# Mixing sublayer: gate, projection and q/k, v/g products with token blocks as the stationary operand

## The chip, the core and the metric

One core of a Trainium2 chip runs the whole program: two decoder layers over 256 tokens with a model width of 1024. The metric is the time of one execution on the device in microseconds; a lower one is better. The core has a TensorE (PE, with its weight loads as PEld), a VectorE (DVE), a ScalarE (ACT), a GpSimd (POOL) and a SyncE (SP), which here only sends off the loads.

## What is computed

Each layer is a token-mixing sublayer and a mixture of experts, each followed by a norm. Cut to what matters here:

```python
z = h @ w_in[l]                      # 1024 -> 10 blocks of 256 columns and 4 gate blocks of 1024
(sc_b, sc_c, sc_x, lru_x, sg_u, sg_v, r_q, r_k, r_v, r_g, *gate_logits) = split(z)
branches = (short_conv(sc_b, sc_c, sc_x), rg_lru(lru_x),
            spatial_gating(sg_u, sg_v), retention(r_q, r_k, r_v, r_g))   # each 256 tokens x 256
merged = 0
for b in range(4):
    merged = merged + sigmoid(gate_logits[b]) * (branches[b] @ branch_proj[l, b])   # 256 -> 1024
mix = merged @ w_out[l]              # 1024 -> 1024
h = layer_norm(ALPHA * h + mix)
h = layer_norm(ALPHA * h + mixture_of_experts(h))    # 32 experts, 2 for a token
```

All of it is in float32. The kernel splits each operand of the mixing products in a leading part (hi) and a rest (lo) and sums three products: hi by hi, hi by lo and lo by hi (`tripled`, lines 328 to 330).

## The kernel before

**Weights and pieces.** The weights lie in memory in chunks of 1 MB (128 partitions by 2048 floats), in the order of use: ten input blocks (q, k, lx, v, g, sv, su, c, x, b), then four rounds of four gate chunks, one chunk of branch projections and, from the second round on, one chunk of the output projection; 34 chunks in a layer, followed by 96 chunks for the experts. SP loads each with one instruction (the first two with four) into a ring of 22 slots of 1 MB, as slots come free; the ring also holds the larger buffers of the sublayer. A chunk is used in four pieces of 512 columns. `do_split` copies a piece to `whi` on ACT and takes the rest to `wlo` on DVE (lines 256 and 257, in `hilo`), four pieces ahead of its products (`LOOK`); `wlo` has four places, so that the split of piece u+4 waits until the products of piece u are done.

**Products.** A piece of an input block or a gate takes 12 matmuls of 256 columns. For q, k, v, g and sv the tokens are stationary (128 tokens by 128 inputs) and 256 weight columns are streamed. For lx, su, c, x, b, the gates and the branch projections the weights are stationary (128 inputs by 128 channels) and the 256 tokens are streamed, so that the result has channels on the partitions. In the output projection the merged rows are stationary and 512 weight columns are streamed (`add_to`).

**Side work.** After each piece `advance` takes one step of every generator that runs beside the products: retention (`g_ret`), the recurrence (`g_lru`), spatial gating (`g_sgu`), the short convolution (`g_sc`), the merge (`g_merge`). What a step sends to PE stands in PE's order behind that piece. Each engine works its instructions off in the order in which the program gives them. Retention starts when q is done: rotations on DVE, an add on POOL, transposes on PE, scores, a standardisation (`std64`) whose inverse root is 12 small POOL instructions in three rounds of four (lines 315 to 318), two POOL products (lines 620 and 621) and, four steps later, the transposes `rtp` (line 628). Spatial gating has the same kind of `std64`, one POOL product (line 697) and then 16 matmuls `sv` (line 705).

**Merge.** For eight blocks of 128 channels and two pairs of branches, a gate bank goes through a sigmoid on ACT (line 401), the projection's bank is multiplied with it on DVE (line 483), and the two pairs are added on POOL (line 488). The sum, with channels on the partitions, is split in hi and lo and is the stationary operand of the output projection as it stands. `residual` scales `h` on POOL beside the gates (line 922; in the second layer lines 927 to 930, after a load of 1 MB), and `g_router` follows with line 291.

Of the kernel before, what the change touches and what calls it, by code (L numbers as in the profile page):

```python
# [39 lines left out]
# columns of the pack of shape constants  # L40
# [13 lines left out]


def _stream():
    s = [("in", n) for n in ("q", "k", "lx", "v", "g", "sv", "su", "c", "x", "b")]
    for m in range(4):
        s += [("gate", 2 * m + j, bp) for j in range(2) for bp in range(2)]
        s.append(("proj", m))  # L60
        if m:
            s.append(("out", m - 1))
    return s + [("out", 3)]


STREAM = _stream()
NMIX = len(STREAM)
# [15 lines left out]
class Ring:  # L83
    """The slots of 1 MB: weights in flight, and the larger buffers while they live."""
# [14 lines left out]
    def pump(self):  # L99
        while self.next < len(self.chunks) and self.free > self.reserve():  # L100
# [3 lines left out]
            if self.next % NCH == NCH - 1:  # L104
                for c in (slice(0, 1024), slice(1024, 2048)):
                    self.k.nc.sync.dma_start(t[:, c], self.chunks[self.next][:, c])
            elif self.next == 0:
                for i in range(4):
                    c = slice(512 * i, 512 * i + 512)
                    self.k.nc.sync.dma_start(self.k.xT[:, 2 * i:2 * i + 2], self.k.a["xT"][:, 2 * i:2 * i + 2])  # L110
                    self.k.nc.sync.dma_start(t[:, c], self.chunks[0][:, c])
            else:
                n = 4 if self.next == 1 else 1
                for i in range(n):
                    c = slice(2048 // n * i, 2048 // n * (i + 1))
                    self.k.nc.sync.dma_start(t[:, c], self.chunks[self.next][:, c])
# [7 lines left out]
class Kern:  # L124
    def __init__(self, ctx, tc, a, out):
# [11 lines left out]
        self.ring.chunks = []  # L137
        for l in range(L):
            self.ring.chunks += [a["mixw"][l, i] for i in range(NMIX)]
            self.ring.chunks += [a["exps"][l, g, i] for g in range(8) for i in range(12)]  # L140
# [42 lines left out]
    def rope_tables(self):  # L183
        """cos, and -sin with sin, of the angles brought to within pi of 0."""
# [69 lines left out]
    def hilo(self, hi, lo, src, eng=None):  # L254
        """hi: the leading bits of src, lo: the rest, exactly."""
# [3 lines left out]
    def params(self, l):  # L259
        """The smaller parameters of a layer's mixers."""  # L260
# [19 lines left out]
    def g_router(self, l):  # L280
        """The norm's gain and bias go into the router's weights and biases; the sums of its weights."""
# [23 lines left out]
    def rsqrt(self, v, n, tag):  # L305
        """v ** -0.5 on [P, n], by Newton's iteration."""
# [16 lines left out]
    def tripled(self, out, pairs, stop_last=True, first=True):  # L323
        """Sum of products of split operands: (lhsT hi, lo), (rhs hi, lo)."""
# [7 lines left out]
    def prologue(self, l):  # L332
        self.base, self.late = l * NCH, None
        self.pieces = [(self.base + c, s) for c in range(NMIX) for s in range(4)]
        self.splits, self.nsplit = {}, 0

    def do_split(self, u, eng=None):
# [8 lines left out]
        if s == 3:  # L346
# [3 lines left out]
    def mixer(self, l):  # L350
# [12 lines left out]
        for kind, *args in STREAM:  # L363
            n = args[0]
            if kind == "in":
                tm = n in TOKENS_FIRST
                bank = self.bank("B", "z")
                for s in range(4):
                    wh, wl = self.splits.pop(u)
                    if tm:  # L370
# [19 lines left out]
            elif kind == "gate":  # L390
                bank = self.bank("B", "z")
                for s in range(4):
                    wh, wl = (x.rearrange("p (k c) -> p k c", k=4) for x in self.splits.pop(u))
                    o = bank[:, (s // 2) * 256:(s // 2) * 256 + 256]
                    self.tripled(o, [((wh[:, kk], wl[:, kk]), hk(4 * (s % 2) + kk)) for kk in range(4)],
                                 stop_last=s % 2 == 1, first=s % 2 == 0)
                    u += 1
                    if s == 3:
                        j, bp = args
                        g = self.late_sub("gate")  # L400
                        nc.scalar.activation(g, bank, AF.Sigmoid)  # L401
                        self.gates[j, bp] = g
                        if (j, bp) == (0, 0):
                            self.residual(l)
                            self.gens.append(self.g_router(l))
                        if (j, bp) == (4, 0) and l:
                            ring.give()
                        if (j, bp) == (7, 1):
                            ring.give(2)
                    self.advance()  # L410
                    self.do_split(u - 1 + LOOK)
            elif kind == "proj":
                for s in range(4):
                    wh, wl = (x.rearrange("p (b k c) -> p b k c", b=2, k=2) for x in self.splits.pop(u))
                    j, bp = 2 * n + s // 2, s % 2
                    bank = self.bank("P", "pj")
                    for b in range(2):
                        bh, bl = (x[:, 2 * bp + b] for x in self.br)
                        self.tripled(bank[:, b * 256:b * 256 + 256],
                                     [((wh[:, b, k], wl[:, b, k]), (bh[:, k], bl[:, k])) for k in range(2)])  # L420
                    u += 1
                    self.mgens.append(self.g_merge(j, bp, bank))
                    self.advance()
                    self.do_split(u - 1 + LOOK)
                if n == 3:
                    ring.give(2)
            else:
                if self.W is None:
                    assert not self.gens
                    self.W = [[self.bank("W", "acc") for _ in range(2)] for _ in range(2)]  # L430
                def add_to(t, half, k, w):
                    mh, ml = self.merged[k]
# [913 lines left out]
```

## Time and profile before

| what | value |
|---|---|
| median of 3 runs | 863.62 us (863.32 to 863.98) |
| the profiled execution, first to last instruction | 860.7 us |
| around it: the median less that span | 2.9 us |
| PE busy | 791.3 us, 92% of the span |
| DVE busy | 386.0 us |
| ACT busy | 317.3 us |
| loads | 281.07 MB, mean 327 GB/s |
| TensorE's mean granted clock | 0.970 of full speed |

The profile is of one execution; its span leaves out what lies ahead of the first and behind the last instruction. A matmul's listed duration holds its way through the array, so that the listed times of neighbours overlap; what a matmul costs in a stream is the distance from its start to the next one's. The granted clock is a share of full speed: 1.00 is 2.4 GHz and 0.50 is 1.2 GHz.

### The profile page before, as it was taken

To read this page: it belongs to the slowest core of one execution; us is meant where nothing else is said; L and a number is where in the kernel's file an instruction comes from. 1 tells how busy PE (TensorE), PEld (TensorE's weight loads), DVE (VectorE), ACT (ScalarE), POOL (GpSimd) and SP (SyncE) were. 2 spreads that over 40 slices of the span, in tenths; PEclk is the share of its full clock that TensorE was granted. 3 is DMA by queue.
4 is the path that set the end of the run, shared out by engine and by line. 5 is a ranking of instruction groups with operands and counts; after the bars stand their busy time and mean duration, and the time that the engine had idled before them with its cause. 6 is when DMAs were issued, how large, how long until landed. Compare 5 with 4: busy or idle time off the path is not lost.

```text
span 860.7 us, 15923 instructions
## 1 busy us (share of the span) xinstructions
PE 791.3 (92%) x6438; PEld 604.1 (70%) x6438; DVE 386.0 (45%) x732; ACT 317.3 (37%) x636; POOL 124.8 (14%) x153
## 2 busy tenths in 40 slices
PE   8999999999999999867889998999999999979794
PEld 7998999999656555422389988999995565544342
DVE  5778677466621111110386779665674211111004
ACT  6564444444523211110356633544444131112012
POOL 4526211011000000000131437110010000000001
PEclk9999999999999999988999999999999999997898
DMA  9986735557799999999997474555587999999994
GB/s 346 425 354 264 253 122 179 191 196 280 323 424 426 426 426 425 425 421 425 424 425 303 158 281 164 183 196 191 175 334 320 426 426 426 425 426 427 423 425 175
DMA packets 40823, 281.07 MB, mean 327 GB/s; under 512 B 4588, under 2 KB 4588, under 8 KB 7456
## 3 DMA queue, kind: packets, MB, share of 16 engines
q1 hardware_dynamic: 40320, 279.20, 80.9%
q8 instruction: 54, 0.88, 0.4%
q10 hardware_dynamic: 288, 0.52, 0.2%
q0 software_dynamic: 128, 0.19, 0.1%
q14 instruction: 33, 0.27, 0.1%
HBM read 278.85 MB, written 1.05 MB: 325 GB/s over the span
## 4 chain that ended last, share of the span: by engine, by line
PE 58%; DMA 27%; DVE 7%; ACT 2%; POOL 1%; issue 1%; SPq 0%; DVEq 0%; ACTq 0%; POOLq 0%
DMA w<-in_exps_dram 25%; PE z L328 9%; PE z L330 9%; PE z L329 9%; PE gu L1052 6%; PE xg L1151 3%; PE y L1102 3%; PE acc L1089 3%; DVE wlo L257 2%; PE pj L330 2%; PE pj L328 2%; PE pj L329 2%; PE acc L328 2%; PE acc L329 2%; PE acc L330 2%; DMA par<-in_par_dram 2%
## 5 line engine op out<-in xcount | busy, mean ns | idle before, releaser
L257 DVE TENSOR_TENSOR wlo<-w,whi 128x512 fp32r<-128x512 f32 x269 | 215.7, 825 | 115.7 <-ACT whi L256 71.6
L330 PE MATMUL z<-hThi,wlo 128*128 128x256 f32 x672 | 192.2, 286 | 3.2 <-DVE wlo L257 3.0
L328 PE MATMUL z<-hThi,whi 128*128 128x256 f32 x672 | 192.5, 286 | 0.4 <-ACT whi L256 0.4
L329 PE MATMUL z<-hTlo,whi 128*128 128x256 f32 x672 | 191.3, 285 | 0.0
L256 ACT CAST whi<-w 128x512 fp32r<-128x512 f32 x272 | 151.4, 618 | 13.4 <-PE z L329 6.7
L1052 PE MATMUL gu<-w,xg 128*32 128x512 f32 x1024 | 128.0, 635 | 22.2 <-PEq L1175 13.0
L330 PEld LDWEIGHTS z<-hThi,wlo 128*128 128x128 f32 x672 | 130.1, 194 | 4.9 <-DVE wlo L257 4.9
L328 PEld LDWEIGHTS z<-hThi,whi 128*128 128x128 f32 x672 | 130.3, 194 | 1.2 <-ACT whi L256 0.7
L329 PEld LDWEIGHTS z<-hTlo,whi 128*128 128x128 f32 x672 | 130.2, 194 | 0.2
L1052 PEld LDWEIGHTS gu<-w,xg 128*32 128x32 f32 x1024 | 30.4, 114 | 98.2 <-issue 65.3
L1157 ACT ACTIVATE xg<-xg,cst 128x128 f32<-128x128 f32 x64 | 25.8, 454 | 167.2 <-PE xg L1151 163.9
L1159 DVE TENSOR_SCALAR xg<-xg,cst 128x128 f32<-128x128 f32 x64 | 23.3, 405 | 129.7 <-PE xg L1151 129.7
L1102 PE MATMUL y<-w,hidT 128*32 128x256 f32 x1024 | 65.4, 383 | 12.8 <-ACT hidT L1082 10.8
L1151 PEld LDWEIGHTS xg<-oh,h 128*128 128x128 f32 x512 | 59.6, 191 | 24.4 <-issue 22.7
L1089 PE MATMUL acc<-y,ct 128*128 128x256 f32 x256 | 68.1, 398 | 1.0 <-ACT y L1106 1.0
L1151 PE MATMUL xg<-oh,h 128*128 128x128 f32 x512 | 65.4, 281 | 0.0
L1089 PEld LDWEIGHTS acc<-y,ct 128*128 128x128 f32 x256 | 44.7, 189 | 25.0 <-issue 11.9
L1102 PEld LDWEIGHTS y<-w,hidT 128*32 128x32 f32 x1024 | 28.9, 109 | 41.1 <-ACT hidT L1082 14.6
L488 POOL TENSOR_TENSOR late<-late 128x512 f32<-128x512 f32 x16 | 25.9, 1616 | 203.9 <-DVE late L483 184.7
L1128 DVE TENSOR_TENSOR ow<-oh,wt 128x256 f32<-128x256 f32 x16 | 6.8, 424 | 106.9 <-PE y L1102 78.8
L1106 ACT COPY y<-y 128x256 f32<-128x256 f32 x64 | 23.8, 373 | 78.6 <-PE y L1102 78.6
L401 ACT ACTIVATE late<-z 128x512 f32<-128x512 f32 x32 | 19.1, 597 | 90.6 <-PE z L330 90.6
(257 smaller groups left out, 1044.4 us busy)
## 6 DMA issues: line engine op xcount, KB each, us to landing
w<-in_exps_dram SPq DMA_DIRECT2D x190, 1024.0 KB, 19.5
w<-in_mixw_dram SPq DMA_DIRECT2D x66, 1024.0 KB, 8.0
w<-in_mixw_dram SPq DMA_DIRECT2D x8, 256.0 KB, 6.2
par<-in_par_dram SPq DMA_DIRECT2D x2, 1024.0 KB, 15.9
w<-in_exps_dram SPq DMA_DIRECT2D x4, 512.0 KB, 17.7
xT<-in_xT_dram SPq DMA_DIRECT2D x4, 256.0 KB, 5.4
h<-in_xtok_dram SPq DMA_DIRECT2D x1, 1024.0 KB, 18.2
gb<-in_fgb_dram SPq DMA_DIRECT2D x1, 1024.0 KB, 5.8
```

The lines of the kernel that those rows point to most:

```text
L256: self.nc.scalar.copy(hi, src)
L257: (eng or self.nc.vector).tensor_sub(lo, src, hi.bitcast(F32))
L328: nc.tensor.matmul(out, ah, bh, start=first and i == 0, stop=False, skip_group_check=True)
L329: nc.tensor.matmul(out, ah, bl, start=False, stop=False, skip_group_check=True)
L330: nc.tensor.matmul(out, al, bh, start=False, stop=stop_last and i == n - 1, skip_group_check=True)
L488: nc.gpsimd.tensor_add(a, a, pr)
L1052: nc.tensor.matmul(bank[32 * c:32 * c + 32], xg[g][k // 4][:, k % 4, 32 * c:32 * c + 32], w[:, c], start=k == 0, stop=k == 7, skip_group_c ...
L1089: nc.tensor.matmul(self.W[t][half][:, c0:c0 + 256], ct[:, t * P:t * P + P], y, start=g == 0 and c0 == 0, stop=g == 7, skip_group_check=True)
L1102: nc.tensor.matmul(bank[32 * c:32 * c + 32], hidT[:, f * P + 32 * c:f * P + 32 * c + 32], w[:, f, c], start=f == 0, stop=f == 1, skip_grou ...
L1106: nc.scalar.copy(ys[q], bank)
L1151: nc.tensor.matmul(bank[:, i * P:i * P + P], self.h[:, t, k * P:k * P + P], oh[:, t].rearrange("p e s -> p (e s)"), start=t == 0, stop=t == 1)
L1157: nc.scalar.activation(x[:, 2 * j + i], bank[:, i * P:i * P + P], AF.Identity, bias=b, scale=g)
```

## The change

The order of the work is written out as a list of units (`_work`), apart from the order in memory, which stays as it is. q and k are one product, and so are v and g: for each of the 8 blocks of 128 inputs the tokens are stationary and 512 columns (256 of each) are streamed. The gates and branch projections do the same with 512 channels of one branch: two halves of the 1024 channels, in each the four branches one after the other, with two chunks of gates and half a chunk of projections each. The four gated projections of a half are added up with tokens on the partitions; then eight blocks are transposed on PE, split in hi and lo, and are the stationary operand of the output projection. Output chunk 0 comes after branch 0 of the second half, the other three at the end. Since a chunk in use now mixes columns of several chunks in memory, `parts` cuts its load: four loads of 256 KB with rows of 1 KB (q/k, v/g) or 512 B (gates), eight of 128 KB with rows of 512 B (projections). Input blocks and gates use the PSUM banks in another order, and the ring's slots are given back at other places.

```diff
-    s = [("in", n) for n in ("q", "k", "lx", "v", "g", "sv", "su", "c", "x", "b")]
-    for m in range(4):
-        s += [("gate", 2 * m + j, bp) for j in range(2) for bp in range(2)]
...
+NAMES = ("qk", "qk", "lx", "vg", "vg", "sv", "su", "c", "x", "b")
...
+    for n, name in enumerate(NAMES):
+        j = NAMES[:n].count(name)
+        work.append((("in", name, j), use("in", name, j)))
+    for hf in range(2):
+        for b in range(4):
+            for kh in range(2):
+                work.append((("gate", hf, b, kh), use("gate", hf, b, kh)))
+            two = (b % 2 * 2, b % 2 * 2 + 1)
+            work.append((("proj", hf, b), use("proj", hf, b // 2, pieces=two)))
+            if (hf, b) == (1, 0):
+                work.append((("out", 0), use("out", 0)))
+    for n in range(1, 4):
+        work.append((("out", n), use("out", n)))
...
+    def parts(self, t, u):
...
+        if kind == "in" and x in PAIRS:
+            at = STREAM.index(("in", x[0]))
+            src = mix[at:at + 2].rearrange("n p (k c) -> p k n c", k=8)[:, 4 * arg[0]:4 * arg[0] + 4]
+            dst = t.rearrange("p (k n c) -> p k n c", k=4, n=2)
+            return [(dst[:, k], src[:, k]) for k in range(4)]
...
+        if kind == "gate":
+            b, kh = arg
+            at = STREAM.index(("gate", 4 * x, b // 2))
+            src = mix[at:at + 4].rearrange("j p (b k c) -> p b k j c", b=2, k=8)[:, b % 2, 4 * kh:4 * kh + 4]
+            dst = t.rearrange("p (k j c) -> p k j c", k=4, j=4)
+            return [(dst[:, k], src[:, k]) for k in range(4)]
...
+        for (kind, n, *args), pieces in WORK:
+            if kind == "in" and n in PAIRS or kind == "gate":
+                kh = args[-1]
+                if kh == 0:
+                    banks = [self.bank("B", "z") for _ in range(2)]
+                for s in range(4):
+                    w = self.splits.pop(u)
+                    k = 4 * kh + s
+                    for t in range(2):
+                        self.tripled(banks[t], [(ht(k, t), w)], stop_last=k == 7, first=k == 0)
+                    u += 1
+                    if k == 7 and kind == "in":
+                        self.z[n] = banks
+                        self.side(l, n)
+                    elif k == 7:
+                        g = self.gates[args[0]] = [self.gate_sub(args[0], t) for t in range(2)]
+                        for t in range(2):
+                            nc.scalar.activation(g[t], banks[t], AF.Sigmoid)
+                        if (n, args[0]) == (0, 0):
+                            self.residual(l)
+                            self.gens.append(self.g_router(l))
...
+                    self.advance()
+                    self.do_split(u - 1 + LOOK)
...
+            elif kind == "proj":
+                b, = args
+                w = [self.splits.pop(u + k) for k in range(2)]
+                banks = [self.bank("P", "pj") for _ in range(2)]
+                for t in range(2):
+                    self.tripled(banks[t], [([x[:, b, k, t * P:t * P + P] for x in self.br], w[k]) for k in range(2)])
+                u += 2
+                self.mgens.append(self.g_merge(n, b, banks))
+                for i in range(2):
                     self.advance()
+                    self.do_split(u - 2 + i + LOOK)
...
+    def g_merge(self, hf, b, banks):
...
+        g = self.gates.pop(b)
+        for t in range(2):
+            nc.vector.tensor_mul(g[t], banks[t], g[t])
+            if b == 0:
+                continue
+            (nc.vector if b == 3 else nc.gpsimd).tensor_add(self.sums[t], self.sums[t], g[t])
...
+        if b < 3:
             return
...
+        yield
+        mT = [self.bank("B" if hf else "W", "mT") for _ in range(2)]
+        for t in range(2):
+            for i in range(4):
+                nc.tensor.transpose(mT[i // 2][:, i % 2 * 256 + t * P:i % 2 * 256 + t * P + P],
+                                    sums[t][:, i * P:i * P + P], self.ident)
+        yield
+        for i in range(2):
+            h, l = store[:, 2 * i], store[:, 2 * i + 1]
+            self.hilo(h, l, mT[i])
...
-        for i, n in enumerate("qk"):
-            z = yield from self.wait(n)
-            A, B = r0[2 * i], r0[2 * i + 1]
...
+        for t, z in enumerate(self.z["qk"]):
+            A, B = r0[2 * t], r0[2 * t + 1]
...
-        yield from self.wait("v")
+        yield from self.wait("vg")
...
-        yield from self.wait("g")
```

## Rows read from the trace of the kernel before

**Rows 1.** Windows: us, busy time (instructions) of each engine, PEclk, DMA share, GB/s.

```profile
100.00:200.00 100.00, 100.00 (x793) 98.08 (x792) 61.24 (x94) 45.92 (x89) 9.69 (x6) 1.00 0.52 176
225.00:235.00 10.00, 8.74 (x71) 5.27 (x73) 5.96 (x34) 5.52 (x10) 0.00 (x0) 1.00 0.58 244
250.00:336.00 86.00, 82.18 (x760) 46.60 (x756) 11.98 (x32) 19.32 (x51) 0.00 (x0) 1.00 1.01 426
```

**Rows 2.** Groups by line and shape on PE: busy us, mean ns, idle before.

```profile
L328 PE MATMUL z<-hThi,whi 128*128 128x256 f32 x672 | 192.5, 286 | 0.4 <-ACT whi L256 0.4
...
L328 PE MATMUL z<-whi,hThi 128*128 128x256 f32 x160 | 47.9, 299 | 2.3 <-ACT whi L256 1.5 <-DVE lru L650 0.7
...
L328 PE MATMUL pj<-br,whi 128*128 128x256 f32 x128 | 36.2, 283 | 0.0
```

**Rows 3.** Timeline of PE, gates: start us, us, engine, line, operation.

```profile
100.08 0.28 PE L330 MATMUL z<-hThi,wlo 128*128 128x256 f32 x1
...
103.80 0.28 PE L328 MATMUL z<-hThi,whi 128*128 128x256 f32 x1
```

**Rows 4.** Timeline of PE, output projection.

```profile
142.30 0.40 PE L328 MATMUL acc<-whi,late 128*128 128x512 f32 x1
...
144.81 0.39 PE L330 MATMUL acc<-whi,late 128*128 128x512 f32 x1
```

**Rows 5.** Timelines of PE, ACT and DVE where a projection follows a gate.

```profile
135.84 0.28 PE L328 MATMUL pj<-br,whi 128*128 128x256 f32 x1
...
136.04 0.60 ACT L401 ACTIVATE late<-z 128x512 f32<-128x512 f32 x1 [3.10 <-PE z L330]
...
137.18 0.69 DVE L257 TENSOR_TENSOR wlo<-w,whi 128x512 fp32r<-128x512 f32 x1 [1.83 <-ACT whi L256]
137.79 0.68 DVE L483 TENSOR_TENSOR late<-pj,late 128x512 f32<-128x512 f32 x1
```

**Rows 6.** Timeline of PE, four transposes and the next product.

```profile
456.38 0.60 PE L584 MATMUL rtp<-cst,ret 128*128 128x128 f32 x4
456.73 0.36 PE L328 MATMUL z<-whi,hThi 128*128 128x256 f32 x1
```

**Rows 7.** Timeline of POOL, two of the six rounds of the inverse roots.

```profile
60.21 0.51 POOL L315 TENSOR_TENSOR rzr<-ryr 128x8 f32<-128x8 f32 x1 [1.84 <-DVE ryr L312]
...
62.03 0.71 POOL L318 TENSOR_TENSOR ryr<-ryr,rzr 128x8 f32<-128x8 f32 x1
...
75.13 0.20 POOL L315 TENSOR_TENSOR rzs<-rys 128x8 f32<-128x8 f32 x1
...
75.98 0.20 POOL L318 TENSOR_TENSOR rys<-rys,rzs 128x8 f32<-128x8 f32 x1
```

**Rows 8.** Timelines of DVE and PE, and a window (PE busy, PEclk, DMA).

```profile
62.60 0.68 DVE L535 TENSOR_REDUCE sas<-sgu 128x8 f32<-128x512 f32 x1
...
73.78 0.66 PE L628 MATMUL rtp<-cst,ret 128*128 128x128 f32 x4 [2.10 <-POOL ret L621]
...
74.00:80.00 6.00, 6.00 (x45) 0.72 0.25 101
```

**Rows 9.** Timelines of POOL, DVE and PE beside the residual's scaling, both layers.

```profile
84.54 5.75 POOL L922 TENSOR_SCALAR h<-h 128x2048 f32<-128x2048 f32 x1
...
84.97 4.73 DVE L257 TENSOR_TENSOR wlo<-w,whi 128x512 fp32r<-128x512 f32 x2
...
520.29 15.29 DVE L257 TENSOR_TENSOR wlo<-w,whi 128x512 fp32r<-128x512 f32 x9
...
532.27 0.38 PE L330 MATMUL z<-hThi,wlo 128*128 128x256 f32 x1 [1.10 <-DVE wlo L257]
```

**Rows 10.** Timelines of PE and ACT, start of the second layer.

```profile
430.37 0.47 PE L328 MATMUL z<-whi,hThi 128*128 128x256 f32 x1
...
436.99 3.93 ACT L256 CAST whi<-w 128x512 fp32r<-128x512 f32 x7
...
438.69 0.39 PE L329 MATMUL z<-wlo,hThi 128*128 128x256 f32 x1 [0.66 <-DVE wlo L257]
```

More of the change, by code (lines that the diff above doesn't have):

```diff
@@ L53, with _work, use @@
 TOKENS_FIRST = ("q", "k", "v", "g", "sv")
+PAIRS = ("qk", "vg")
+NAMES = ("qk", "qk", "lx", "vg", "vg", "sv", "su", "c", "x", "b")
 def _stream():
     s = [("in", n) for n in ("q", "k", "lx", "v", "g", "sv", "su", "c", "x", "b")]
-    for m in range(4):
-        s += [("gate", 2 * m + j, bp) for j in range(2) for bp in range(2)]
[L60 to L63, printed above, removed]
+    for hf in range(2):
+        s += [("gate", 4 * hf + j, bp) for bp in range(2) for j in range(4)]
+        s += [("proj", 2 * hf + m) for m in range(2)]
+    return s + [("out", n) for n in range(4)]
+def _work():
+    s, work, at = [], [], {}
+    def use(*key, pieces=range(4)):
+        if key not in at:
+            at[key] = len(s)
+            s.append(key)
+        return [(at[key], i) for i in pieces]
+    for n, name in enumerate(NAMES):
+        j = NAMES[:n].count(name)
+        work.append((("in", name, j), use("in", name, j)))
+    for hf in range(2):
+        for b in range(4):
[7 more added lines that the diff above has]
+        work.append((("out", n), use("out", n)))
+    return s, work
 STREAM = _stream()
+LOADS, WORK = _work()
 NMIX = len(STREAM)
@@ L103, in pump @@
             t = self.take("w")
[L104 to L111, printed above, removed]
-            else:
[L113 to L116, printed above, removed]
+            dma = self.k.nc.sync.dma_start
+            parts = self.k.parts(t, self.next)
+            if self.next == 0:
+                for i, (dst, src) in enumerate(parts):
+                    dma(self.k.xT[:, 2 * i:2 * i + 2], self.k.a["xT"][:, 2 * i:2 * i + 2])
+                    dma(dst, src)
+            else:
+                for dst, src in parts:
+                    dma(dst, src)
             self.tiles[self.next] = t
@@ L333, in prologue @@
         self.base, self.late = l * NCH, None
-        self.pieces = [(self.base + c, s) for c in range(NMIX) for s in range(4)]
-        self.splits, self.nsplit = {}, 0
+        self.pieces = [(self.base + c, s) for _, pieces in WORK for c, s in pieces]
+        self.splits, self.nsplit, self.whole = {}, 0, {}
     def do_split(self, u, eng=None):
@@ L345, in do_split @@
         self.splits[u] = hi, lo
-        if s == 3:
+        self.whole[c] = self.whole.get(c, 0) + 1
+        if self.whole[c] == 4:
             del self.ring.tiles[c]
@@ L362, in mixer @@
         u = 0
[L363 to L367, printed above, removed]
+        tags = {"lx": "P", "sv": "P", "su": "B", "c": "P", "x": "B", "b": "P"}
+        for (kind, n, *args), pieces in WORK:
[19 more added lines that the diff above has]
+                            self.gens.append(self.g_router(l))
+                        if (n, args[0]) == (1, 0) and l:
+                            ring.give()
+                        if (n, args[0]) == (1, 3):
+                            ring.give(2)
+                    self.advance()
+                    self.do_split(u - 1 + LOOK)
+            elif kind == "in":
+                bank = self.bank(tags[n], "z")
                 for s in range(4):
                     wh, wl = self.splits.pop(u)
-                    if tm:
+                    if n == "sv":
                         wh, wl = (x.rearrange("p (k c) -> p k c", k=2) for x in (wh, wl))
@@ L389, in mixer @@
                     self.advance()
[L390 to L409, printed above, removed]
-                    self.advance()
[L411 to L426, printed above, removed]
@@ new lines, in mixer @@
+            elif kind == "proj":
[7 more added lines that the diff above has]
+                for i in range(2):
+                    self.advance()
+                    self.do_split(u - 2 + i + LOOK)
+                if (n, b) == (1, 3):
+                    ring.give()
@@ L456, in mixer @@
                     self.advance()
-        assert not self.splits
+        assert not self.splits and not self.mgens
         next(norm, None)
@@ L460, in mixer @@
         self.needs[l] = int(l + 1 == L)
-        ring.give(3)
+        ring.give(4)
     def advance(self):
@@ L515, in side @@
             self.gens.append(self.g_sc(l))
-        elif n == "v":
-            self.nc.scalar.copy(self.r1[2], self.z["v"])
-        elif n == "g":
+        elif n == "vg":
+            for t in range(2):
+                self.nc.scalar.copy(self.r1[2][:, 256 * t:256 * t + 256], self.z["vg"][t][:, :256])
             self.gens.append(self.g_silu())
```

85 lines of the change are left out of this document (46 added, 39 removed).

## The prediction

> **What bounds the kernel now.** First the windows, for the stages. In the middle of a mixing sublayer PE is busy for the whole 100 us at full clock, while DMA has 0.52 of its time taken: the sublayer goes at PE's pace. Between sublayer and experts DMA falls to 0.58 because the ring is full; from 250 us on it is at 1.01 and 426 GB/s and PE waits for it [rows 1]. So the experts' stage starts when the sublayer's PE work ends, with a full ring, and then takes a fixed number of bytes: what a sublayer gains or loses on PE moves the end by the same amount, once a layer. Next the groups by shape and the timeline of PE, for what a product costs; then DVE, ACT and POOL at the places where PE would have to wait for them.
>
> **What the streaming saves.** Of the 672 products of a kind with weights stationary, 512 belong to gates (16 chunks of 16, two layers), the other 160 to lx, su, c, x and b, which stay. Of the 160 with tokens stationary, 128 belong to q, k, v and g. With the 128 projections that makes 768 of each of three kinds [rows 2], 2,304 products of 256 columns, which become 1,152 of 512. In a stream a product of 256 columns takes (103.80 - 100.08) / 31 = 0.120 us [rows 3], one of 512 columns with its own stationary load takes (144.81 - 142.30) / 11 = 0.228 us [rows 4]. The sum is 2,304 x 0.120 - 1,152 x 0.2282 = 276.5 - 262.9 = **13.6 us saved**; a piece goes from 1.44 to 1.37 us. The other number of columns is not an extrapolation: the output projection already runs in this shape.
>
> The Trainium skill speaks against it: TensorE: Matmul & The Clock Gate, Back-to-back issue gap, gives an isolated product N / 2.4 + 2.5 ns, by which a pair of 256 costs 218 ns and one of 512 costs 216. By that only 1,152 x 2.5 ns = 2.9 us would be saved and the sum below would end 10.7 us higher. The rows show 240 against 228, and I go by them.
>
> **What the merge adds.** Before, the sums came out with channels on the partitions and PE never waited for them. Now 8 transposes for each half stand in PE's order directly behind the last projection of the half, and they need both gated sums. Four transposes hold up the next product by 456.73 - 456.38 = 0.35 us [rows 6]. For the wait I set the start of a projection at 0, by the place where one follows a gate now [rows 5]: it starts at 135.84, the sigmoid 0.20 later, the next split's copy behind it, its subtraction on DVE at 1.34, the first gate product at 1.95. The first of the two sigmoids now waits for a bank that ends 0.68 earlier, so that the second one keeps this place. DVE then has: product 1.95, add 2.66, product 3.27, add 3.98 to 4.67 (0.68 each, 0.03 more where one needs the other). PE ends its 12 products at 2.74, starts the first four transposes at 3.45, the second four at 4.77 and is free at 5.12. So each merge costs 5.12 - 2.74 = 2.4 us, 1.7 of it waiting; four of them **9.5 us**. At best DVE has no split ahead and the chain starts when the first bank is done, at 1.6: 2.0 us each, 8 in all. At worst a POOL instruction slows one of the DVE operations, as it does elsewhere (0.69 to 1.7 us, [rows 5, 9]): 3.4 each, 13.6 in all. I take 9.5, as POOL is idle there. What is queued behind the transposes is the next gate or output piece, whose split is already made; it loses nothing more. The other merges (branches 0 to 2) are the same two DVE products and two POOL adds with a gate's 11 us to spare.
>
> **What moves: retention.** Before, its scores came after v, at step 17; now after v and g, at step 21, and everything of it that follows comes four pieces later. Its inverse root then falls on the same steps (31 to 33) as that of spatial gating, and POOL works six rounds in one row. A round took 2.53 us where DVE was busy (60.21 to 62.74) and 1.05 where it was not (75.13 to 76.18) [rows 7]; I take 1.75, near the middle, 10.5 us for six. Before, PE waited 2.10 us at `rtp`, until 73.78; so piece 36 ended at 71.68, and by 1.44 us a piece piece 30 ended at 63.0 and piece 27 at 58.7, while gating's reduction for step 27 ran at 62.60, DVE being 3.9 late [rows 8]. Without retention's part ahead of it DVE is some 2 us late, 1.1 us have been saved by then, and two reductions of 0.68 come first: the rounds run from 63.0 - 1.1 + 2 + 1.4 = 65.3 to 75.8, gating's product on POOL ends some 0.7 later (an estimate, less than half such a round), and `sv`, whose place is behind piece 38 at 71.68 + 2.88 - 1.1 = 73.5, waits for it **3.0 us** in place of the 2.1 at `rtp`, which now comes late enough. Both waits are followed by a lower clock: 0.72 over 6 us, for a part of them the 1.2 GHz of the two levels, 1.7 us lost [rows 8]. So I count **+1.0 us a layer, 2.0**. Bounds: all rounds at 1.05 leave no wait and no fall of the clock (-3.8 a layer); all at 2.53 give 15.2 and a wait of 7.7 (+5.6 a layer).
>
> **What moves: the residual.** While POOL scales `h`, a split on DVE takes 2.4 us (first layer) or 1.7 us (second) instead of 0.69 [rows 5, 9]. In the first layer POOL starts as soon as its queue is empty, as before, but retention's last subtraction now lies in that stretch: 2.4 us of DVE more, of which I take half to be covered by the pieces split ahead: **+1.3**. In the second the load is sent off four pieces later, so that the stretch holds a merge (two products, 1.4 us) and 11 splits that are needed 0.07 us sooner each: **+2.2** on top of waits like the one of 1.10 us now [rows 9]. Bounds: 0, if the lookahead covers all, to 7.
>
> **The start of the second layer.** A piece now needs only one block of `hT` and lasts 1.37 us, so PE doesn't run out of them; but the fourth split is needed after three blocks instead of six: 430.37 + 3 x 1.37 = 434.5, and its copy still starts at 436.99, its rest is ready at 438.69 [rows 10]. PE stands for 3 us or more at once and then has five pieces left where it had five already; the 0.5 us saved are outweighed by a fall of the clock as at `rtp` (1.7): **+1.2**, between -0.5 and 1.7.
>
> **At nothing:** the loads in short rows and their many more issues (SP does nothing else, DMA has 48% free in this stage [rows 1]); the other PSUM banks; the four large hi/lo splits for eight small ones; projection chunks and one buffer held longer in a ring that is full anyway. If that cover is gone, the third rival is the price.
>
> **Sum:** -13.6 + 9.5 + 2.0 + 3.5 + 1.2 = +2.6 us: a profiled span of 863.3 for 860.7 and, with 2.9 us around it, **866.2 us** for the median of 863.6.
>
> **Rivals.**
> 1. *POOL is in time* (faster). One place, the inverse roots: nothing else wants DVE while they run, so that the rounds go at the quick rate. It decides if six rounds and gating's product take under 8 us (1.2 a round). Then neither `sv` nor `rtp` waits and the clock stays: 866.2 - 2 x (3.0 + 1.7) = 856.8. For it: rounds of 1.05 and DVE less behind than before; against: rounds of 2.53, and two reductions that now fall together [rows 7, 8].
> 2. *The clock falls at the merges too* (slower): 4 x 1.7 = 6.8 on top, 873.0. Against it: the waits are two short ones, 0.7 and 1.0 us, not one of 2.1 [rows 8].
> 3. *The short rows starve PE* (slower). A gate chunk is used up in 24 x 0.228 = 5.5 us, and at 426 GB/s 1 MB takes 2.5. The free 48 us of 100 [rows 1] spread over the 20 cut chunks of that stage leave 4.9 us for each; at 5.5 us (190 GB/s) the lack is 12 us a layer, 890. The Trainium skill (DMA: Bandwidth & Descriptors, Rules for kernel authors) asks for 1 MB or more in one load for full bandwidth, and these are 128 to 256 KB; no row shows such a load in this stage.
> 4. *The streaming saves nothing* because a product of 512 with its load costs two of 256 here: 879.8. The rows of the output projection speak against it [rows 4]. By the rule of the Trainium skill above it would be 876.9.
>
> **How the numbers follow.** Forecast (own range 861 to 870) 0.43; rival 1 0.31; rival 2 0.15; rival 3 0.06; rival 4 0.05. A measurement of this kernel can tell about 0.2% (1.7 us) from no change. Faster: rival 1 and 0.06 of the forecast's lower end, 0.37. Same (861.9 to 865.3): 0.18, all of the forecast. Slower: the forecast's other 0.19 and rivals 2 to 4, 0.45. The range, 855 to 876, takes in rivals 1 and 2 and leaves out most of 3 and 4.
>
> **What would show it.** Products of 512 columns 0.228 apart; at four places PE's transposes wait for DVE's add, some 1.7 us each; one wait of 2 to 4 us at `sv` and none at `rtp`; waits for `wlo` beside the residual; a wait of 3 us near 435 us; DMA's share in the gates well under 1. Wrong would be: no wait at `sv`, a granted clock under 1 behind the merges, or PE waiting for loads.

## The result, and the profile after

The changed kernel takes 868.69 us (median of 4 runs, 867.33 to 869.85); the kernel before took 863.80 us (863.32 to 864.97) beside it. The ratio is 1.0060, with a 95% interval of 1.0046 to 1.0074: slower by 0.6%, 4.9 us, where 866.2 us had been forecast. The profiled execution has a span of 865.6 us, against 860.7.

The page of the changed kernel, its number of instructions and the busy time of each engine, and then three of its windows, which answer to [rows 1]:

```profile
span 865.6 us, 13977 instructions
...
PE 783.2 (90%) x5318; PEld 545.8 (63%) x5318; DVE 376.4 (43%) x718; ACT 326.1 (38%) x632; POOL 121.8 (14%) x153
```

```profile
100.00:200.00 100.00, 98.60 (x439) 81.05 (x438) 64.39 (x90) 49.14 (x85) 11.98 (x8) 1.00 0.54 185
225.00:235.00 10.00, 8.78 (x84) 6.28 (x83) 6.74 (x38) 4.88 (x11) 0.00 (x0) 1.00 0.52 205
250.00:336.00 86.00, 82.77 (x756) 46.76 (x744) 11.99 (x32) 18.93 (x50) 0.00 (x0) 1.00 1.01 426
```

PE has 8 us less to do, yet the span is longer. In the middle of the sublayer PE is no longer busy throughout (1.4 us missing, one merge), and the experts' stage starts with DMA held back and then runs at 426 GB/s, as before.

**The stream.** Two products of the gates that lie nine apart, on PE's timeline; (151.10 - 149.06) / 9 = 0.227 us, against 0.228 in [rows 4]:

```profile
149.06 0.39 PE L381 MATMUL z<-whi,hThi 128*128 128x512 f32 x1
...
151.10 0.39 PE L381 MATMUL z<-whi,hThi 128*128 128x512 f32 x1
```

**The merge.** PE at the first merge, and then DVE with the two products and sums that PE waits for; they answer to [rows 5, 6]:

```profile
141.31 0.39 PE L383 MATMUL pj<-whi,br 128*128 128x512 f32 x1
142.36 0.66 PE L554 MATMUL mT<-cst,late 128*128 128x128 f32 x4 [0.66 <-DVE late L540]
143.75 0.66 PE L554 MATMUL mT<-cst,late 128*128 128x128 f32 x4 [0.74 <-DVE late L540]
144.16 0.48 PE L381 MATMUL z<-whi,hThi 128*128 128x512 f32 x1
```

```profile
140.82 0.69 DVE L537 TENSOR_TENSOR late<-pj,late 128x512 f32<-128x512 f32 x1
141.61 0.69 DVE L540 TENSOR_TENSOR late<-late 128x512 f32<-128x512 f32 x1
142.22 0.68 DVE L537 TENSOR_TENSOR late<-pj,late 128x512 f32<-128x512 f32 x1
143.00 0.69 DVE L540 TENSOR_TENSOR late<-late 128x512 f32<-128x512 f32 x1
```

PE was free at 142.36 - 0.66 = 141.70 and goes on at 144.16: 2.46 us a merge by PE's idle time. Counted from start to start, as the prediction counts, the next product would have begun at 141.31 + 0.23 = 141.54, and a merge costs 2.62 us. The clock stays at 1.00.

**Retention and gating on POOL.** The first and the last of the six rounds, and gating's product, on POOL; then `sv` on PE, and PE's busy time, granted clock and DMA behind it in both layers (windows of PE alone). They answer to [rows 7, 8]:

```profile
65.73 0.20 POOL L368 TENSOR_TENSOR rzr<-ryr 128x8 f32<-128x8 f32 x1 [4.47 <-DVE ryr L365]
...
76.07 0.20 POOL L371 TENSOR_TENSOR rys<-rys,rzs 128x8 f32<-128x8 f32 x1
76.35 1.04 POOL L761 TENSOR_TENSOR sgu<-sgu,rys 128x512 f32<-128x512 f32 x1
```

```profile
77.45 2.03 PE L769 MATMUL sv<-par,sgu 128*64 128x128 f32 x16 [4.16 <-POOL sgu L761]
...
503.10 2.03 PE L769 MATMUL sv<-par,sgu 128*64 128x128 f32 x16 [4.15 <-POOL sgu L761]
```

```profile
77.00:83.00 6.00, 5.55 (x31) 0.52 1.14 340
503.00:510.00 7.00, 6.90 (x35) 0.54 0.42 158
```

PE waits 4.2 us in each layer and then runs at the lower of its two clocks (1.2 GHz). At a mean of 0.52 over 6 us of which 5.55 were worked some 2.7 us are lost, and 7 x 0.46 = 3.2 us in the second layer. There is no wait at `rtp`.

**The residual.** PE's waits beside the residual, first layer, then second; then splits on DVE, one of the first layer and six of the second, and the windows of the second layer's clock. They answer to [rows 9]:

```profile
89.99 0.50 PE L382 MATMUL z<-wlo,hThi 128*128 128x512 f32 x1 [1.22 <-DVE wlo L310]
93.36 0.50 PE L382 MATMUL z<-wlo,hThi 128*128 128x512 f32 x1 [0.32 <-DVE wlo L310]
...
536.77 0.50 PE L382 MATMUL pj<-wlo,br 128*128 128x512 f32 x1 [0.83 <-DVE wlo L310]
539.55 0.50 PE L382 MATMUL pj<-wlo,br 128*128 128x512 f32 x1 [1.80 <-DVE wlo L310]
```

```profile
85.81 4.13 DVE L310 TENSOR_TENSOR wlo<-w,whi 128x512 fp32r<-128x512 f32 x1
...
528.78 12.76 DVE L310 TENSOR_TENSOR wlo<-w,whi 128x512 fp32r<-128x512 f32 x6 [0.50 <-issue]
```

```profile
530.00:540.00 10.00, 7.37 (x32) 5.48 (x31) 10.00 (x5) 3.99 (x7) 9.84 (x5) 1.00 0.49 140
540.00:550.00 10.00, 10.00 (x39) 8.06 (x38) 7.76 (x11) 3.73 (x6) 3.35 (x3) 0.83 0.95 280
```

In the first layer one split is held up for 4.13 us and those behind it take 0.7 us again. In the second a split takes 12.76 / 6 = 2.1 us, DVE is not idle from 530 to 540 us, and behind the last wait the clock falls (0.83 over 10 us, 1.7 us).

**Start of the second layer.** PE's timeline; it answers to [rows 10]:

```profile
438.68 0.49 PE L381 MATMUL z<-whi,hThi 128*128 128x512 f32 x1 [2.69 <-ACT whi L309]
439.71 0.50 PE L382 MATMUL z<-wlo,hThi 128*128 128x512 f32 x1 [0.54 <-DVE wlo L310]
```

### The profile page after: what moved, and what is told of

Read it like the earlier page. It is cut to its first block, busy times and chain, and to the rows that moved or that the text cites. A ratio compares the mean times of both kernels' runs of the same rounds, so it can differ in the third digit from the quotient of the medians.

```text
span 865.6 us, 13977 instructions
## 1 busy us (share of the span) xinstructions
PE 783.2 (90%) x5318; PEld 545.8 (63%) x5318; DVE 376.4 (43%) x718; ACT 326.1 (38%) x632; POOL 121.8 (14%) x153
## 4 chain that ended last, share of the span: by engine, by line
PE 29%; DMA 20%; DVE 4%; ACT 1%; POOL 1%; issue 1%; ACTq 0%; DVEq 0%; SPq 0%; POOLq 0%
DMA w<-in_exps_dram 18%; PE z L381 5%; PE z L382 5%; PE z L383 5%; PE gu L1116 3%; DMA w<-in_mixw_dram 2%; PE xg L1215 2%; PE y L1166 1%; PE acc L1153 1%; PE acc L381 1%; PE acc L383 1%; PE acc L382 1%; DVE wlo L310 1%; PE pj L382 1%; PE pj L383 1%
## 5 line engine op out<-in xcount | busy, mean ns | idle before, releaser
L310 DVE TENSOR_TENSOR wlo<-w,whi 128x512 fp32r<-128x512 f32 x269 | 207.6, 795 | 129.2 <-ACT whi L309 59.6
L309 ACT CAST whi<-w 128x512 fp32r<-128x512 f32 x272 | 159.0, 621 | 87.5 <-PE z L383 51.1
L381 PE MATMUL z<-whi,hThi 128*128 128x512 f32 (+1 forms) x352 | 137.1, 389 | 5.4 <-ACT whi L309 5.4
L382 PE MATMUL z<-wlo,hThi 128*128 128x512 f32 (+1 forms) x352 | 135.1, 384 | 2.8 <-DVE wlo L310 2.8
L383 PE MATMUL z<-whi,hTlo 128*128 128x512 f32 (+1 forms) x352 | 134.2, 381 | 0.0
L381 PEld LDWEIGHTS z<-whi,hThi 128*128 128x128 f32 x352 | 66.7, 190 | 20.3 <-ACT whi L309 7.5
L1166 PE MATMUL y<-w,hidT 128*32 128x256 f32 x1024 | 66.0, 386 | 13.6 <-ACT hidT L1146 10.8
L382 PEld LDWEIGHTS z<-wlo,hThi 128*128 128x128 f32 x352 | 66.7, 190 | 17.4 <-DVE wlo L310 5.3
L383 PEld LDWEIGHTS z<-whi,hTlo 128*128 128x128 f32 x352 | 66.5, 189 | 13.1 <-DVE hTlo L962 0.4
L383 PE MATMUL z<-hThi,wlo 128*128 128x256 f32 x160 | 46.5, 291 | 1.4 <-DVE wlo L310 1.4
L381 PE MATMUL z<-hThi,whi 128*128 128x256 f32 x160 | 47.0, 294 | 0.0
```

The lines of the kernel that those rows point to most:

```text
L309: self.nc.scalar.copy(hi, src)
L310: (eng or self.nc.vector).tensor_sub(lo, src, hi.bitcast(F32))
L381: nc.tensor.matmul(out, ah, bh, start=first and i == 0, stop=False, skip_group_check=True)
L382: nc.tensor.matmul(out, ah, bl, start=False, stop=False, skip_group_check=True)
L383: nc.tensor.matmul(out, al, bh, start=False, stop=stop_last and i == n - 1, skip_group_check=True)
L1166: nc.tensor.matmul(bank[32 * c:32 * c + 32], hidT[:, f * P + 32 * c:f * P + 32 * c + 32], w[:, f, c], start=f == 0, stop=f == 1, skip_grou ...
```

## The experiments

Each ratio is to the kernel before, on the same chip. The changed kernel's is 1.0060, and a thousandth is 0.86 us: a ratio r lies (r - 1.0060) x 864 us from the changed kernel. The intervals reach 1 to 1.5 us to either side, those of runs 1, 5, 7 and 8 some 2 to 2.6 us; that of the changed kernel's own ratio, 1.2 us, comes on top where a run is set against it.

**1. The streaming alone taken back** (`e5_halves`)

```diff
-self.tripled(banks[t], [(ht(k, t), w)], stop_last=k == 7, first=k == 0)
+for j in range(2):
+    c = slice(256 * j, 256 * j + 256)
+    self.tripled(banks[t][:, c], [(ht(k, t), [x[:, c] for x in w])], stop_last=k == 7, first=k == 0 and j == 0)
```

> The changed kernel with the streaming alone taken back: each product of 512 columns of gates, projections, q with k and v with g is issued as two of 256 with the same stationary block; everything else stays. Theory (a product of 256 takes 0.120 us, one of 512 takes 0.228): 1,152 x (0.240 - 0.228) = +13.6 on PE; the slower pieces give POOL and DVE some 0.07 us more a piece, so waits shrink by 1 to 3 us: 879 to 882.5. Rival (512 columns cost two times 256, the fourth rival of the prediction): 868 to 869.

881.17 us, ratio 1.0222 (1.0197 to 1.0247): 14.0 us slower than the changed kernel. Two products of the gates that lie fifteen apart on PE's timeline of this kernel; (151.68 - 149.88) / 15 = 0.120 us:

```profile
149.88 0.28 PE L381 MATMUL z<-whi,hThi 128*128 128x256 f32 x1
...
151.68 0.28 PE L381 MATMUL z<-whi,hThi 128*128 128x256 f32 x1
```

So the stream of 512 columns is worth what the spacings said, and the rival by which it saves nothing falls.

**2. Retention's normalisation later** (`e1_ret_later`)

```diff
+for _ in range(6):
+    yield
 d = r1[0]
 rs = yield from self.std64(bank, d, r1[1], "r")
```

> The changed kernel with one edit: retention's normalisation starts six pieces later, so that its three rounds on POOL come behind gating's and not between them. Theory (the six rounds in one row make the wait at sv, 4.2 us a layer, and the half clock behind it, 3.4 us a layer): no wait at sv, granted clock 1.00 between 70 and 90 us, 868.7 - 2 x 7.6 = 853.5 us. Rival A (gating is late for DVE's sake, because of its own reductions): the wait at sv stays above 2 us, 864 or more. Rival B (the wait only moves to rtp): one wait of 3 us or more at rtp, 868.

862.92 us, 1.0004 (0.9992 to 1.0016): 4.8 us faster, a third of what the theory gave. `sv` does not wait any more, the clock is 1.00 from 60 to 80 us, and gating's three rounds, begun at 64.8, end at 69.9. But POOL now comes to the residual while DVE has more to do. POOL, DVE and PE of this kernel there, each from its timeline:

```profile
83.11 5.69 POOL L988 TENSOR_SCALAR h<-h 128x2048 f32<-128x2048 f32 x1
...
83.49 4.12 DVE L310 TENSOR_TENSOR br<-sgu,br 128x512 fp32r<-128x512 f32 x1
...
88.27 0.50 PE L382 MATMUL z<-wlo,hThi 128*128 128x512 f32 x1 [2.98 <-DVE wlo L310]
```

One subtraction that takes 0.69 us elsewhere takes 4.12 beside POOL's 5.69, the split behind it is late, and PE waits 2.98 us (before that 0.9). Beside the residual PE now waits 3.9 us in the first layer and 6.0 in the second, where it waited 1.5 and 2.6. The theory was right about the cause of the wait, and wrong that its price comes back: more than half of what is missing went into these waits. It had also set the low clock at 3.4 us a layer, which is more than the trace of the changed kernel (2.7 and 3.2) and run 12 (1.5) give. Neither rival had named that place.

**3. The transposes two pieces later** (`e2_tr_later`)

```diff
-yield
+for _ in range(3):
+    yield
 mT = [self.bank("B" if hf else "W", "mT") for _ in range(2)]
```

> The changed kernel with one edit: the transposes of a half's merged sums are issued two pieces later. Theory (the waits of 0.66 and 0.74 us before them are the merge's price, the eight transposes themselves the rest, 0.9 us or so): the four waits go, -4 x 1.4 = -5.6, 863.1 us. Rival (PE would have to wait for something else in these pieces, a split or a bank of PSUM, or the transposes are the greater part): 867 or more.

861.64 us, 0.9987 (0.9976 to 0.9999): 6.3 us faster. The waits are gone, the eight transposes stand in one row on PE. Of 4 x 2.46 = 9.8 us that leaves 3.5 us for the transposes themselves; on PE's timeline of this kernel eight of them begin at 144.32 and the next product at 145.11, 4 x 0.79 = 3.2 us.

**4. The fourth split earlier** (`e3_split4`)

```diff
 if a == 0:
     self.do_split(2, G)
+if a == 2:
+    self.do_split(3)
```

> The changed kernel with one edit: the fourth split of the second layer's first chunk is made before the fifth block of hT, not after the eighth. Theory (PE's wait of 2.69 us near 436 us is for this split alone): the wait goes, -2.5 us, 866.2 us. Rival (what is moved back, the last blocks of hT, is late in its stead, or the next split is): the wait stays at 2 us or more, at hT or at the fifth split, 868.5 us.

868.58 us, 1.0073 (1.0058 to 1.0088): no gain. The rival holds: PE now stands one piece later, for the fifth split. PE's timeline of this kernel:

```profile
439.27 0.49 PE L381 MATMUL z<-whi,hThi 128*128 128x512 f32 x1 [1.92 <-ACT whi L309]
440.30 0.50 PE L382 MATMUL z<-wlo,hThi 128*128 128x512 f32 x1 [0.54 <-DVE wlo L310]
```

The fifth piece can go on at 439.27 + 0.54 = 439.8; in the changed kernel the fourth one begins at 438.68, waits 0.54 more, takes 1.37, and the fifth follows at 440.6. Of the 2.5 us expected 0.8 are left, and the timed runs do not show them. In the trace they are used up at once, because the clock falls behind the wait; it did not in the profiled execution of the changed kernel (1.00 over the same window). The window of this kernel:

```profile
440.00:445.00 5.00, 4.70 (x14) 3.71 (x15) 3.20 (x6) 2.73 (x6) 0.00 (x0) 0.66 1.02 429
```

**5. The residual issued earlier** (`e4_resid`): the call moved from the end of the first gate to its middle.

```diff
+if kind == "gate" and (n, args[0], k) == (0, 0, 3):
+    self.residual(l)
...
 if (n, args[0]) == (0, 0):
-    self.residual(l)
     self.gens.append(self.g_router(l))
```

> The changed kernel with one edit: the residual (POOL scales h; in the second layer it also sends for gain and bias) is issued after the first half of the first gate, four pieces earlier, where the kernel before has it. Theory (in the second layer the stretch would be over before the first merge and end its waits of 0.83 and 1.80 us and the lower clock behind them, in the first layer nothing changes): -2 to -4 us, 865.7. Rival (POOL starts when its queue is empty, whatever the order, and the same number of splits meets it): 868 to 869.

867.94 us, 1.0062 (1.0039 to 1.0085): no change. The waits in the second layer only move (1.6 us at `pj`, 1.1 us at `z` in place of 2.6 us at `pj`).

**6. Dense loads** (`e6_dense`): the weights lie in memory in the order of the chunks.

```diff
-return [(dst[:, k], src[:, k]) for k in range(4)]
+return [(t, self.a["mixw"][l, n])]
```

> The changed kernel with the weights of the mixing sublayer laid out so that each chunk is one load of 1 MB with long rows again (the first two chunks in four loads, as in the kernel before). Theory (short rows cost something at the start alone, where PE waits 1.22, 0.99 and 0.54 us for loads): -0.6 to -1.5 us, 867.5. Rival A (they slow the loads of the whole stage and with them PE or other transfers): -4 us or more. Rival B (they cost nothing anywhere): within 0.3 us.

867.70 us, 1.0052 (1.0035 to 1.0070): 0.7 us faster, as the theory had it, but not to be told from rival B, nothing at all. The windows of 20 to 50 us and of 40 to 45 us, of the changed kernel and then of this one:

```profile
20.00:50.00 30.00, 30.00 (x198) 26.90 (x197) 19.25 (x38) 20.62 (x37) 15.97 (x33) 1.00 0.97 364
40.00:45.00 5.00, 5.00 (x42) 4.66 (x42) 2.53 (x4) 4.67 (x10) 2.35 (x2) 1.00 0.99 296
```

```profile
20.00:50.00 30.00, 30.00 (x198) 26.90 (x197) 19.19 (x38) 20.63 (x37) 16.06 (x33) 1.00 1.01 425
40.00:45.00 5.00, 5.00 (x42) 4.66 (x41) 2.43 (x4) 4.62 (x11) 2.43 (x3) 1.00 1.01 426
```

In the first part of the long window (20 to 36 us) loads of 1 MB are still among those of the changed kernel, and both get some 425 GB/s. From 36 to 46 us it sends for cut loads only; DMA is taken up in both, and the short rows bring 296 GB/s where the long ones bring 426. That is still above the 190 GB/s of rival 3 in the prediction, and PE is busy throughout: loads run far enough ahead.

**7. The kernel before, `rtp` later** (`e7_before_rtp`)

```diff
-for _ in range(4):
+for _ in range(8):
     yield
 bank = self.bank("W", "rtp")
```

> The kernel before with one edit: the transposes of retention's result are issued four pieces later. Theory (the kernel before pays a wait of 2.1 us at rtp and the clock behind it, 1.7 us, in each layer): 863.6 - 2 x 3.8 = 856.0 us. Rival (the wait moves to another place): 863.

868.88 us, 1.0067 (1.0043 to 1.0092): 5.8 us slower than the kernel before, which neither had expected. PE and POOL of this kernel, and then of the kernel before, each from its timeline:

```profile
79.18 1.72 PE L705 MATMUL sv<-par,sgu 128*64 128x128 f32 x16 [4.26 <-POOL sgu L697]
...
78.08 1.04 POOL L697 TENSOR_TENSOR sgu<-sgu,rys 128x512 f32<-128x512 f32 x1
```

```profile
78.73 1.15 PE L705 MATMUL sv<-par,sgu 128*64 128x128 f32 x16
...
76.26 1.04 POOL L697 TENSOR_TENSOR sgu<-sgu,rys 128x512 f32<-128x512 f32 x1
```

With `rtp` out of the way PE comes to `sv` earlier, at 74.9 us. POOL does not; its product even ends later, at 79.1 us for 77.3, as two small instructions of its last rounds take 0.92 us each for 0.2 to 0.3. The wait at `sv` (4.3 us, and 4.2 in the second layer) is twice the one removed. So most of this wait lay in the kernel before too; its wait of 2.1 us at `rtp` and the low clock behind it had hidden it, as PE came to `sv` 1.4 us after POOL was done.

**8. Three edits at once** (`e8_all`): 2, 3 and 4 together.

> The changed kernel with three edits at once: retention's normalisation six pieces later, the transposes of the merged sums two pieces later, the fourth split earlier. If each of the theories holds and they add up: 868.7 - 15.2 - 5.6 - 2.5 = 845.4 us, faster than both kernels. If the waits only move about: 860 or more.

854.51 us, 0.9911 (0.9881 to 0.9940): 12.9 us faster than the changed kernel and faster than both. The single edits as measured give 4.8 + 6.3 - 1.1 = 10.0; the 2.9 us more are not clear of the intervals. It is a good half of what the theories gave. Beside the residual PE still waits 3.8 us in the first layer and 6.0 in the second.

**9. The residual off POOL** (`e10_resid_off`). `residual` becomes a generator that is advanced once a piece: ACT scales, DVE multiplies and adds, 512 columns at a time.

```diff
-nc.gpsimd.tensor_scalar(self.h, self.h, ALPHA, None, op0=OP.mult)
+for q in range(4):
+    x = gb[:, 512 * q:512 * q + 512] if l else self.h[:, q // 2, q % 2 * 512:q % 2 * 512 + 512]
+    nc.scalar.activation(x, x, AF.Identity, scale=ALPHA)
+    yield
...
-nc.gpsimd.tensor_mul(self.h[:, t], self.h[:, t], gb[:, :1024])
-nc.gpsimd.tensor_add(self.h[:, t], self.h[:, t], gb[:, 1024:])
+nc.vector.tensor_mul(x, x, gb[:, c:c + 512])
+yield
+yield
+nc.vector.tensor_add(x, x, gb[:, 1024 + c:1536 + c])
```

> The changed kernel with one edit: the residual taken off POOL as in the kernel with the other edits. Theory (here PE waits 1.22 and 0.32 us in the first layer and 0.83 and 1.80 us in the second beside the residual, and 1.8 us of clock are lost behind the last): -6.0 us, 862 us, the waits at sv and at the merges unchanged. Rival (these splits are late for the wait at sv, not for POOL): the waits stay, 867 or more.

860.55 us, 0.9976 (0.9961 to 0.9991): 7.3 us faster. No wait is left beside the residual, while `sv` (4.1) and the merges (0.7 each) wait as before. DVE got more work and has no more trouble: it was POOL's long instructions, not DVE's load. The edit changes two things at once, the engine and the cutting into pieces; no run has POOL do the same work in pieces of 512 columns.

**10. All of it** (`e9_all_resid_off`): edits 2, 3 and 9.

> The changed kernel with retention's normalisation six pieces later, the transposes of the merged sums two pieces later, and the residual taken off POOL: its scaling on ACT in pieces of 512 columns, in the second layer products and sums on DVE, one for two pieces of weights. Theory (what the first two edits should have given and did not is lost where the residual's long POOL instructions hold up DVE's splits: waits of 3.0 and 0.8 us in the first layer, 3.0, 0.8 and 2.2 us in the second, about 1.7 us of lower clock behind each group): 854.5 - 9.8 - 3.4 = 841 us. Rival (DVE is behind in this stretch by its own load, to which 5.5 us are added here): waits for splits of 3 us or more stay, 850 or more.

842.64 us, 0.9771 (0.9757 to 0.9784): 25.0 us faster than the changed kernel, 2.3% faster than the kernel before, and the fastest version of all. Its windows over both stretches:

```profile
60.00:100.00 40.00, 39.19 (x249) 33.70 (x247) 33.03 (x58) 22.65 (x40) 16.52 (x30) 1.00 1.00 298
480.00:560.00 80.00, 79.18 (x409) 65.75 (x408) 63.80 (x100) 41.37 (x72) 20.82 (x32) 1.00 0.74 237
```

PE lacks 0.8 us in each, and the clock holds there. The 25.0 us are also the sum of what each edit removes if none is eaten: 8.4 us of waits at `sv`, 3.0 of clock (run 12), 6.3 at the merges, 7.3 beside the residual; the four numbers are not known so well that the sum must come out to the tenth. What is left is the start of the second layer: waits of 2.66 and 0.54 us, and a clock of 0.57 from 428 to 432 us behind them.

**11. The kernel before, with the same care** (`e11_before_tuned`): `rtp` and `sv` four pieces later, the residual off POOL.

```diff
-for _ in range(3):
+for _ in range(7):
     yield
 bank = self.bank("W", "sv")
```

> The kernel before with the transposes of retention's result and the products with sv both issued four pieces later, and the residual taken off POOL in the same way. Theory (POOL's rounds are late for rtp and, once rtp does not wait, for sv: with both places moved behind the end of POOL's work neither waits): -2 x (2.1 + 1.7) and some 3 us of waits for splits in the second layer: 863.6 - 10.6 = 853 us; the stream of 512 columns and the transposes behind the sums would then be worth what is left between this kernel and the changed one with its three edits. Rival (the waits move once more): 860 or more.

852.94 us, 0.9883 (0.9868 to 0.9899): 10.1 us faster than the kernel before. With these waits out of both kernels the change is worth 852.94 - 842.64 = 10.3 us (measured side by side), near the 13.6 of streaming less 3.5 of transposes. The start of the second layer is still against it: in the traces of the two kernels waits of 3.2 us and a lower clock, against 2.2 us and a clock of 1.00.

**12. PE kept at work before `sv`** (`e12_warm`): 18 products more, which nothing reads.

```diff
+self.keep_warm(18)
 bank = self.bank("W", "sv")
```

> The changed kernel with 18 products that nothing reads (bf16, 512 columns, some 0.22 us each) put in PE's order directly before the products with sv, so that PE works through most of its wait of 4.2 us there; what POOL does is the same. Theory (a part of the price of this wait is the lower clock behind it, 1.7 to 3.4 us a layer, and not the wait alone): granted clock 1.00 from 70 to 90 us, the products with sv begin where they did, -2 x 1.7 to -2 x 3.4 us: 862 to 865.3. Rival (the clock falls for another reason, or what it costs is hidden by other waits): 868 to 869.

864.31 us, 1.0025 (1.0014 to 1.0036): 3.0 us faster with no work taken away. PE's timeline, and windows of this kernel:

```profile
73.33 4.06 PE L203 MATMUL warm<-ones 128*128 128x512 bf16 x18
77.64 1.15 PE L770 MATMUL sv<-par,sgu 128*64 128x128 f32 x16 [0.25 <-POOL sgu L761]
```

```profile
70.00:80.00 10.00, 9.75 (x74) 7.15 (x73) 4.80 (x11) 1.24 (x2) 8.80 (x19) 1.00 1.04 303
80.00:90.00 10.00, 8.54 (x41) 6.71 (x40) 8.71 (x10) 2.83 (x6) 7.04 (x2) 1.00 0.88 257
```

`sv` begins 0.2 us later than in the changed kernel, takes 1.15 us where it took 2.03, and the clock holds. The lower clock behind the wait is a cost of its own: 1.5 us a layer in the timed runs, which is what is left after the next waits, beside the residual, grew by 0.25 us a layer in the trace.

## Why the prediction was right

The forecast was 2.5 us too low, in its own range (861 to 870), and the likeliest case was the one that came. By its terms:

- **Streaming, -13.6:** 14.0 (run 1), with 0.227 us for a product. Rival 4 and the reading of the Trainium skill (TensorE: Matmul & The Clock Gate, Back-to-back issue gap) by which a pair of 256 costs nearly what one of 512 does fall with it: in run 1, where the gates' products have 256 columns again, they are 0.120 us apart again.
- **Merges, +9.5:** 4 x 2.46 = 9.8 by PE's idle time, 4 x 2.62 = 10.5 from start to start; counted in this second way, which is the prediction's, the waits are 0.8 and 1.0 us where 0.7 and 1.0 had been foreseen. Rival 2 falls: no clock is lost there.
- **Retention and gating on POOL, +2.0:** the mechanism was right, the size was not. The rounds ran from 65.7 to 76.3 us (foreseen: 65.3 to 75.8), but gating's product took 1.04 us for 0.7, and the wait was 4.2 us for 3.0. Against the 2.1 us at `rtp` that is +4.1 in both layers. The clock, set at 1.7 us as in [rows 8], cost 1.5 a layer in the timed runs (run 12), and 2.7 and 3.2 in the profiled execution. Rival 1 (POOL in time) falls.
- **Residual, +3.5:** PE's waits in this stretch grew from 0.4 to 1.5 us in the first layer and from 2.2 to 2.6 in the second, and 1.7 us of clock are new: +3.2. The sum was right by luck: half of it came from the clock, which had not been counted there, and the waits of the second layer grew by 0.4 us where 2.2 had been foreseen. The 2.4 us for a split in the first layer was a mean of two, and hid that one is held up for some 4 us and the next hardly at all.
- **Start of the second layer, +1.2:** waits of 3.2 us for 2.3, +0.9. The fall of the clock in this term did not come in the profiled execution; in that of run 5, with the same wait of 2.7 us, the clock stood at 0.83 from 440 to 450 us, 1.7 us. It came in the profiled executions of all ten other versions of the changed kernel and in none of the three of the kernel before and its versions, so that the timed runs probably hold it: +2.6 rather than +0.9.
- **Short rows, 0:** right to 0.7 us (run 6); rival 3 falls.

Together -14.0 + 9.8 + 4.1 + 3.2 + 0.9 = +4.0 us, with 4.9 measured. This sum leaves out the clock behind `sv`, 2.5 us more in the profiled execution than the two times 1.7 us behind `rtp`, and the clock at the start of the second layer, 1.7 us. So the terms account for the measured difference to some 3 us, and that the sum comes closer is luck.

What the prediction had not seen is how these terms hang together. It priced the wait at `rtp` as a cost of the kernel before that the change takes away. Run 7 shows that this wait was the cover of another one, and run 2 that the wait at `sv` covers the one at the residual in the same way. So the single terms can add up to the time of the two kernels as they stand and still not tell what an edit gives back: taking away the wait at `sv` gave a third of its price (run 2), while the merges' waits (run 3) and the residual's (run 9) came back whole.

## What to carry to other kernels

Where one engine works through a chain that several places of another engine's order wait for, the waits cover each other: price what the next place would wait if this one did not, before counting a removed wait as a gain. Look for a cause that several of them share; here it is POOL's work beside DVE's splits, and taking the residual off POOL gave 7.3 us alone and let the other edits keep theirs. A gain that a change loses to such waits is still in it: with these waits out of both kernels the change is worth -10 us, not +5.

## What the runs showed of the hardware

**POOL and DVE.** An instruction on DVE that reads two operands from SBUF is held up by a long one on POOL: 4.12 us for 0.69 in run 2. One that reads its large operand from PSUM is not: 0.43 us each beside POOL in run 8, 0.44 in run 2 with POOL idle. DVE and then POOL in run 8, from their timelines:

```profile
513.59 0.86 DVE L699 TENSOR_SCALAR ret<-rtp,cst 128x256 f32<-128x256 f32 x2
514.37 2.11 DVE L310 TENSOR_TENSOR wlo<-w,whi 128x512 fp32r<-128x512 f32 x1
```

```profile
513.08 2.85 POOL L998 TENSOR_TENSOR h<-h,gb 128x1024 f32<-128x1024 f32 x1
```

The Trainium skill has this rule (SBUF — State Buffer, Who interferes with whom): a DVE instruction with two SBUF inputs contends with a GpSimd instruction that reads SBUF. The rows agree. The Trainium skill adds on the same page (SBUF — State Buffer, Summary: rules for kernel authors) that the second one to issue waits until the first has finished. In run 8 the split ends 0.55 us after POOL's instruction, which agrees; in run 2 the subtraction ends at 87.61 us and POOL's scaling, by the profile, at 88.80, which does not.

**The clock.** Behind the wait of 4.2 us the granted clock of the changed kernel stood at 0.50 (1.2 GHz) from 78 to 81 us; eighteen products that nothing reads kept it at 1.00. After the same wait the low clock lasted differently long in different executions: it cost 1.7 us in the profile of run 5 (0.91 and 0.92 over 70 to 90 us) and 2.7 us in that of the changed kernel.

**Short rows.** With DMA taken up, loads cut into 128 and 256 KB with short rows brought 296 GB/s (40 to 45 us), whole ones 426.
